# Rotating an 8192 x 8192 matrix: the last macro tile divided by rows, its loads emitted ahead of its outputs

## Chip, cores, metric

One core of a Trainium2 chip. The metric is the device time of one execution in microseconds. Times are medians over executions unless a profile is named; a profile is one execution, and its own span is about 1.8 us shorter than the time that is counted for it. In the profiles PE is TensorE (PEld its weight loads), DVE is VectorE, ACT is ScalarE, POOL is GpSimd and SP is SyncE; "ACTq" is the part of ACT that issues transfers.

## The reference

```python
def setup_inputs():
    return {"x": np.random.randn(8192, 8192).astype(np.float32), "k": 1}

def reference(x, k):
    return np.rot90(x, k)
```

With k = 1 the output is out[i, j] = x[j, 8191 - i]: a transpose with the columns taken from right to left. 268 MB are read and 268 MB written, and no arithmetic is done.

## The kernel before

The matrix is handled in macro tiles of 1024 rows and 4096 columns. One macro tile is eight loads of 128 rows (2 MB each, 16 KB in a row). VectorE reverses the columns inside each block of 128 into chunks `ar`, PE transposes the blocks into PSUM (the memory that PE writes to), ACT copies two PSUM halves into an output tile, and ACT issues a store of 2 MB: 4 column blocks (G = 4), 128 partitions, rows of 1024 elements (4 KB).

```python
a_pool = tile_pool(bufs=2)      # load buffers, 16 KB a partition
r_pool = tile_pool(bufs=68)     # reversed chunks; a macro tile needs 64
o_pool = tile_pool(bufs=2)      # output buffers, 16 KB a partition
psum_pool = tile_pool(bufs=2, space=PSUM)
...
for r0, c0, C in tiles:
    last = (r0, c0, C) == tiles[-1]
    ...                          # eight loads into a_pool, VectorE copies into chunks[t, j]
    for g0 in range(0, C // P, G):
        if last and g0 // G % 2 == 0:
            ot = a_pool.tile([P, W], dt, tag="a")     # no load needs it any more
        else:
            ot = o_pool.tile([P, W], dt, tag="o")
        S = PW if last and g0 + G == C // P else G
        for h in range(0, G, PW):
            ps = psum_pool.tile([P, PW, R], f32)
            for w in range(PW):
                for t in range(RT):                   # all eight rows of blocks
                    nc.tensor.transpose(ps[:, PW - 1 - w, t * P : (t + 1) * P],
                                        chunks[t, ...], ident)
            nc.scalar.copy(o[:, G - PW - h : G - h, :], ps[:])
            if (h + PW) % S == 0:
                nc.scalar.dma_start(out=dst, in_=...)
```

(Cut; "..." marks what is left out.) An output group needs a block of every one of the eight loads. So the first store of a macro tile cannot start before the eighth load of it has landed and is reversed. In the middle of the run the stores of the tile before cover that wait. Behind the last tile nothing follows, and at its beginning the loads have ended.

## Time and profile before

| | before |
|---|---|
| time | 1271.75 us (1271.64 to 1271.89, 4 executions) |
| span of the profile | 1269.2 us (its execution took 1270.97 us) |
| DMA engines at 9 tenths or more | 39 of 40 slices |
| PE / ACT / VectorE busy | 56% / 37% / 28% |
| last load landed | 1218.00 us |
| first store of the last macro tile issued | 1225.15 us |

From the page of the profile of before: the line of busy engines, the transfer queues (packets, MB, share of the 16 DMA engines' time) and the chain of waits that ended last.

```profile
PE 708.7 (56%) x4096; PEld 668.1 (53%) x4096; DVE 355.2 (28%) x1024; ACT 467.2 (37%) x257; POOL 0.7 (0%) x6
...
q10 hardware_dynamic: 18576, 268.44, 49.8%
q1 hardware_dynamic: 18432, 268.44, 49.8%
...
DMA 78%; ACT 18%; DVE 1%; PE 1%; issue 1%; ACTq 0%; DVEq 0%
```

The stores (q10) and the loads (q1) share the 16 DMA engines and fill 99.6% of their time together. No compute engine is near its limit. A gain is to be sought in stretches in which the DMA engines have nothing to do.

Such stretches are at the end. The same profile in windows; the last three columns are PE's granted clock (as a share of its full speed), the mean busy share of the DMA engines and GB/s.

```profile
core 0: us, PE busy (x) PEld busy (x) DVE busy (x) ACT busy (x) POOL busy (x), PEclk, DMA share, GB/s
1200.00:1213.00 13.00, 5.84 (x32) 5.60 (x32) 4.01 (x12) 4.68 (x3) 0.00 (x0) 0.74 1.01 429
1213.00:1217.00 4.00, 0.98 (x7) 0.74 (x7) 0.00 (x0) 2.59 (x2) 0.00 (x0) 0.78 0.63 264
1217.00:1221.50 4.50, 2.93 (x14) 2.93 (x15) 2.77 (x8) 0.71 (x1) 0.00 (x0) 0.50 0.97 411
1221.50:1226.00 4.50, 4.29 (x37) 4.05 (x36) 0.00 (x0) 3.23 (x3) 0.00 (x0) 0.93 0.05 22
1226.00:1230.00 4.00, 3.43 (x32) 3.15 (x31) 0.00 (x0) 3.43 (x2) 0.00 (x0) 1.00 0.93 393
1230.00:1250.00 20.00, 17.10 (x148) 15.76 (x147) 0.00 (x0) 17.18 (x10) 0.00 (x0) 1.00 1.02 428
```

From 1221.5 to 1226 the engines moved 22 GB/s: a hole of about 4.5 us. What ACT, which makes and issues the stores, did there (start, duration, instruction, and in brackets how long ACT was idle before and what ended it):

```profile
1211.95 3.63 ACT L137 COPY ot<-ps 128x2048 f32<-128x2048 f32 x2 [6.19 <-DMA out_dram<-ot]
1215.62 0.55 ACTq L145 DMA_DIRECT2D out_dram<-ot  x1
1220.79 1.87 ACT L137 COPY ot<-ps 128x2048 f32<-128x2048 f32 x1 [5.20 <-PE ps L132]
1223.25 1.87 ACT L137 COPY ot<-ps 128x2048 f32<-128x2048 f32 x1 [0.60 <-PE ps L132]
1225.15 0.55 ACTq L145 DMA_DIRECT2D out_dram<-ot  x1
```

The store issued at 1215.62 is the last of the tile before. ACT then waits 5.20 us for PE, because PE waits for the last load (landed at 1218.00) and its reversal. The first store of the last tile is issued at 1225.15 and its packets start at 1226.4.

### The profile page before, as it was taken

To read this page: it belongs to the slowest core of one execution; us is meant where nothing else is said; L and a number is where in the kernel's file an instruction comes from. 1 tells how busy PE (TensorE), PEld (TensorE's weight loads), DVE (VectorE), ACT (ScalarE), POOL (GpSimd) and SP (SyncE) were. 2 spreads that over 40 slices of the span, in tenths; PEclk is the share of its full clock that TensorE was granted. 3 is DMA by queue.
4 is the path that set the end of the run, shared out by engine and by line. 5 is a ranking of instruction groups with operands and counts; after the bars stand their busy time and mean duration, and the time that the engine had idled before them with its cause. 6 is when DMAs were issued, how large, how long until landed. Compare 5 with 4: busy or idle time off the path is not lost.

```text
span 1269.2 us, 10385 instructions
## 1 busy us (share of the span) xinstructions
PE 708.7 (56%) x4096; PEld 668.1 (53%) x4096; DVE 355.2 (28%) x1024; ACT 467.2 (37%) x257; POOL 0.7 (0%) x6
## 2 busy tenths in 40 slices
PE   1465645655556555665566555564555555655564
PEld 0364545645555455554556545554555555545564
DVE  4422322232223222232223222332223322232210
ACT  0333334333433343333433333333433343333454
POOL 0000000000000000000000000000000000000000
PEclk9968687776777867767767677677676877768787
DMA  9999999999999999999999999999999999999989
GB/s 400 415 431 429 429 428 429 430 428 429 428 429 428 430 430 428 429 429 430 428 428 420 429 429 429 429 429 427 428 422 427 426 421 430 427 427 427 428 342 382
DMA packets 37057, 537.55 MB, mean 424 GB/s; under 512 B 4112, under 2 KB 4112, under 8 KB 4112
## 3 DMA queue, kind: packets, MB, share of 16 engines
q10 hardware_dynamic: 18576, 268.44, 49.8%
q1 hardware_dynamic: 18432, 268.44, 49.8%
q8 instruction: 32, 0.52, 0.2%
q14 instruction: 17, 0.14, 0.0%
HBM read 268.44 MB, written 268.44 MB: 423 GB/s over the span
## 4 chain that ended last, share of the span: by engine, by line
DMA 78%; ACT 18%; DVE 1%; PE 1%; issue 1%; ACTq 0%; DVEq 0%
DMA out_dram<-ot 72%; ACT ot L137 18%; DMA a<-in_x_dram 6%; DVE ar L111 1%; PE ps L132 1%; ACTq L145 0%; ACTq L137 0%; DVEq L111 0%
## 5 line engine op out<-in xcount | busy, mean ns | idle before, releaser
L132 PE MATMUL ps<-ident,ar 128*128 128x128 f32 x4096 | 708.7, 353 | 544.3 <-ACT ot L137 461.5
L132 PEld LDWEIGHTS ps<-ident,ar 128*128 128x128 f32 x4096 | 668.1, 188 | 584.6 <-ACT ot L137 492.4
L137 ACT COPY ot<-ps 128x2048 f32<-128x2048 f32 x256 | 465.9, 1869 | 747.0 <-DMA out_dram<-ot 724.2
L111 DVE COPY ar<-a 128x512 f32<-128x512 f32 x1024 | 355.2, 421 | 865.7 <-DMA a<-in_x_dram 731.6
L137 ACT ACT_TABLE_LOAD x1 | 1.3, 1283 | 41.1 <-DVE ar L111 41.1
masks.py:199 POOL TENSOR_SCALAR_AFFINE_SELECT ident<-ident 128x128 f32<-128x128 f32 x1 | 0.3, 292 | 0.1
masks.py:197 POOL MEMSET ident<- 128x128 f32 x1 | 0.2, 204 | 0.3 <-POOLq L164 0.3
L164 POOL MEMSET const-bfloat16-1.0<- 128x1 bf16 x1 | 0.1, 101 | 0.0
L164 POOL MEMSET const-uint8-127<- 128x1 uint8 x1 | 0.1, 101 | 0.0
L164 POOL MEMSET const-float32-0.0<- 128x1 f32 x1 | 0.1, 98 | 0.2 <-issue 0.2
L164 POOL MEMSET const-float32-1.0<- 128x1 f32 x1 | 0.1, 98 | 0.0
## 6 DMA issues: line engine op xcount, KB each, us to landing
a<-in_x_dram SPq DMA_DIRECT2D x128, 2048.0 KB, 16.8
out_dram<-ot ACTq DMA_DIRECT2D x127, 2048.0 KB, 15.8
out_dram<-ot ACTq DMA_DIRECT2D x2, 1024.0 KB, 12.6
```

Source lines behind the costliest of these rows:

```text
L111: nc.vector.tensor_copy(out=ar[:], in_=a[:, u, j * CH : (j + 1) * CH].rearrange("r (b m) -> r b m", m=P)[:, :, ::-1],)
L132: nc.tensor.transpose(ps[:, PW - 1 - w, t * P : (t + 1) * P], chunks[t, g * P // CH][:, g % (CH // P), :], ident,)
L137: nc.scalar.copy(o[:, G - PW - h : G - h, :], ps[:])
L164: nc = _bacc.Bacc("TRN2", target_bir_lowering=False, num_devices=1)
```

## The change

The intent: divide the last macro tile into 768 and 256 rows, so that the first part's outputs need only six of the eight loads, and so go out while the last two land. All eight loads are emitted first, so that no load waits for a buffer that an output took. Outputs of the last tile use output and load buffers in turn, now beginning with an output buffer. The core of the diff (cut):

```diff
-LAST = [4096]
+LAST = [6, 2]
 ...
-    for r0, c0, C in tiles:
-        last = (r0, c0, C) == tiles[-1]
+    def load(r0, rt, c0):          # rt loads and their reversals
+    def store(r0, rt, c0, chunks, end, first):
+        rows = rt * P              # 1024, 768 or 256
+        PW = 1
+        while 2 * PW * rows <= FP: PW *= 2
+        G = PW
+        while 2 * G * rows <= F: G *= 2
 ...
-            if last and g0 // G % 2 == 0:
+            if end and (i + first) % 2 == 0:
                 ot = a_pool.tile(...)
 ...
+    *most, before_last, last = tiles
+    for m in most:
+        store(*m, load(*m), False, 0)
+
+    c1 = load(*before_last)        # rows 0..767 of the tile
+    c2 = load(*last)               # rows 768..1023
+    store(*before_last, c1, True, 1)
+    store(*last, c2, True, 1)
```

The first part gives eight stores of 1.5 MB in rows of 3 KB (ACT copies of 128x1536), the second one store of 2 MB and two of 1 MB in rows of 1 KB. Up to the last store of the tile before, the order of instructions on every engine is what it was.

More of the change, by code (lines that the diff above doesn't have):

```diff
@@ L16 @@
 RT = R // P
-LAST = [4096]
+LAST = [6, 2]
 W = 4096
 CH = 512
-G = 4
-PW = 2
+F = 4096
+FP = 2048
 def whole_reads(nc):
@@ L47, in macro_tiles @@
 def macro_tiles(N, M):
-    for r0 in range(0, N, R):
-        widths = [W] * (M // W)
-        if r0 + R == N:
-            widths[-1:] = LAST
-        c0 = 0
-        for C in widths:
-            yield r0, c0, C
-            c0 += C
+    tiles = [(r0, RT, c0) for r0 in range(0, N, R) for c0 in range(0, M, W)]
+    r0, _, c0 = tiles.pop()
+    for n in LAST:
+        tiles.append((r0, n, c0))
+        r0 += n * P
+    return tiles
 @with_exitstack
@@ L83 @@
     )
-    tiles = list(macro_tiles(N, M))
     loads = 0
-    for r0, c0, C in tiles:
-        last = (r0, c0, C) == tiles[-1]
-        q = W // C
+    def load(r0, rt, c0):
+        nonlocal loads
         chunks = {}
-        for t0 in range(0, RT, q):
+        for t in range(rt):
             if loads < RT and loads % 4 >= 2:
@@ L98 @@
             loads += 1
-            a = a.rearrange("r (q c) -> r q c", q=q)
             nc.sync.dma_start(
-                out=a,
-                in_=x[r0 + t0 * P : r0 + (t0 + q) * P, c0 : c0 + C].rearrange(
-                    "(q r) c -> r q c", q=q
-                ),
-            )
-            for u in range(q):
-                for j in range(C // CH):
-                    ar = r_pool.tile([P, CH // P, P], dt, tag="ar")
-                    nc.vector.tensor_copy(
-                        out=ar[:],
-                        in_=a[:, u, j * CH : (j + 1) * CH].rearrange(
-                            "r (b m) -> r b m", m=P
-                        )[:, :, ::-1],
-                    )
-                    chunks[t0 + u, j] = ar
@@ L119 @@
-        for g0 in range(0, C // P, G):
-            if last and g0 // G % 2 == 0:
-                ot = a_pool.tile([P, W], dt, tag="a")
-            else:
-                ot = o_pool.tile([P, W], dt, tag="o")
-            o = ot.rearrange("m (g f) -> m g f", g=G)
-            S = PW if last and g0 + G == C // P else G
+                out=a[:], in_=x[r0 + t * P : r0 + (t + 1) * P, c0 : c0 + W]
+            )
+            for j in range(W // CH):
+                ar = r_pool.tile([P, CH // P, P], dt, tag="ar")
+                nc.vector.tensor_copy(
+                    out=ar[:],
+                    in_=a[:, j * CH : (j + 1) * CH].rearrange(
+                        "r (b m) -> r b m", m=P
+                    )[:, :, ::-1],
+                )
+                chunks[t, j] = ar
@@ new lines, in load @@
+        return chunks
+    def store(r0, rt, c0, chunks, end, first):
+        rows = rt * P
+        PW = 1
+        while 2 * PW * rows <= FP:
+            PW *= 2
+        G = PW
+        while 2 * G * rows <= F:
+            G *= 2
+        for i, g0 in enumerate(range(0, W // P, G)):
+            if end and (i + first) % 2 == 0:
+                ot = a_pool.tile([P, F], dt, tag="a")
+            else:
+                ot = o_pool.tile([P, F], dt, tag="o")
+            o = ot[:, : G * rows].rearrange("m (g f) -> m g f", g=G)
+            S = PW if end and r0 + rows == N and g0 + G == W // P else G
@@ L127 @@
             for h in range(0, G, PW):
-                ps = psum_pool.tile([P, PW, R], mybir.dt.float32)
+                pt = psum_pool.tile([P, FP], mybir.dt.float32, tag="ps")
+                ps = pt[:, : PW * rows].rearrange("m (g f) -> m g f", g=PW)
                 for w in range(PW):
                     g = g0 + h + w
-                    for t in range(RT):
+                    for t in range(rt):
                         nc.tensor.transpose(
@@ L136 @@
                         )
-                nc.scalar.copy(o[:, G - PW - h : G - h, :], ps[:])
+                nc.scalar.copy(o[:, G - PW - h : G - h, :], ps)
                 done = h + PW
@@ L141 @@
                     top = M - c0 - (g0 + done) * P
-                    dst = out[top : top + S * P, r0 : r0 + R].rearrange(
+                    dst = out[top : top + S * P, r0 : r0 + rows].rearrange(
                         "(g m) f -> m g f", g=S
@@ L147 @@
                     )
+    tiles = macro_tiles(N, M)
+    *most, before_last, last = tiles
[5 more added lines that the diff above has]
+    store(*last, c2, True, 1)
 _INS = ['x', 'k']
```

## The prediction

> **What bounds the kernel now.** The transfers. The page's slices show the DMA engines at 9 tenths or more in 39 of 40 slices, at about 428 GB/s; PE is busy 56%, ACT 37%, DVE 28%; the chain of waits is 78% DMA. The Trainium skill ("DMA: Bandwidth & Descriptors", "Where 436 GB/s comes from") puts the ceiling of the 16 engines at 435 GB/s; this trace agrees with 428 to 430 in steady slices. 537 MB at 428 GB/s is about 1255 us of the 1269.2 us span, so no schedule can win over about 14 us (1.1%).
>
> **The loss at the end.** In one-microsecond windows the queues run full to about 1213.5 us, about half full from 1214 to 1218 (last load dripping in), full to 1221.7, near empty until 1226.3, then full to 1266; a straggling engine's packets end at 1267.8. The hole is 4.6 us. By the timeline: the last load lands at 1218.00, VectorE reverses it, PE transposes at half clock, ACT copies end at 1225.1, and only then is the last tile's first store issued (1225.15; its packets start at 1226.4).
>
> **What the change does.** The order of instructions on each engine up to the last store of the tile before is the same. The first part needs only six of the eight loads, the sixth landed at 1198.4, so its first store no longer waits for the last load. It waits for an output buffer instead: that of the second-last store of the tile before, landing at 1219.83. Then two ACT copies of 128x1536 instead of 128x2048: the big ones take 1.87 us, I estimate 1.44 us (by elements, with 0.16 us fixed). First new store issued at about 1222.8, packets at about 1224.0, 2.4 us earlier. The straggling engine ends the store before at about 1224.3, so on it about 2 us are won. The half-rate stretch stays.
>
> After that a 1.5 MB store takes about 3.67 us at 428 GB/s, and ACT's cadence is about 3.46 us (4.31 us now, less two times 0.43): just enough to keep the queue fed. Output buffers come in turn from both pools and are free in time.
>
> **What it costs.** The last 4 MB go out in rows of 1 KB, 12 MB in rows of 3 KB, instead of 4 KB. The skill (same page, "Specifications") asks for at least 512 B; no run here shows 1 KB yet. Loads with 16 KB rows take 611 ns a 16 KB packet, stores of 4 KB rows 615, so the cost of a row seems small; I estimate 0.2 to 1 us in all. Two more store issues (0.55 us) on ACT hide behind the queue.
>
> **Sum.** 1271.8 - 2.1 + 0.4 = 1270.1 us. 8 in 10: 1268.3 to 1272.0. Chances: faster by over 2% 0.003, within 2% 0.99, slower 0.007.
>
> **What would show it.** The first 128x1536 copy starts at about 1219.9, its wait ended by a landing store, not by PE; first new store near 1222.8; near-empty windows only from 1221.7 to 1224; 430 GB/s after; packets of the last three stores at 615 to 650 ns.
>
> **What would make it wrong.** Slow 1 KB rows (packets of 700 ns or more: the gain is gone); PE at half clock, so that ACT waits for it and the queue runs dry between the 1.5 MB stores; the straggling engine carrying its lag to the end, so that little is won.

## The result, and the profile after

| | before | changed |
|---|---|---|
| first measurement | 1271.75 us (1271.64 to 1271.89, 4) | 1270.13 us (1270.06 to 1271.06, 4) |
| again, on another chip | 1271.07 us (1270.39 to 1272.25, 9) | 1270.28 us (1269.53 to 1271.32, 5) |

The ratio is 0.9989 with a 95% interval of 0.9972 to 1.0006, and 0.9993 (0.9980 to 1.0005) the second time. A ratio is the mean time of one kernel's fast runs over that of the other's fast runs of the same rounds, so not quite the ratio of the medians above. Both intervals contain 1: by times alone the gain of about 1 us is not separated from the spread between executions. What happened inside has to be read from the traces.

The profile of the changed kernel is that of its slowest execution (1271.06 us; its span is 1269.2 us, as before, so this pair of profiles shows no gain in time). The same windows:

```profile
1200.00:1213.00 13.00, 5.74 (x37) 5.26 (x35) 3.71 (x11) 4.96 (x3) 0.00 (x0) 0.87 1.01 425
1213.00:1217.00 4.00, 3.40 (x16) 3.40 (x17) 0.00 (x0) 2.31 (x2) 0.00 (x0) 0.58 0.49 205
1217.00:1221.50 4.50, 1.39 (x12) 1.16 (x11) 2.77 (x8) 1.80 (x2) 0.00 (x0) 0.88 0.96 408
1221.50:1226.00 4.50, 4.50 (x23) 4.50 (x22) 0.00 (x0) 2.42 (x2) 0.00 (x0) 0.50 0.57 240
1226.00:1230.00 4.00, 3.64 (x27) 3.34 (x25) 0.00 (x0) 2.71 (x2) 0.00 (x0) 0.84 0.58 246
1230.00:1250.00 20.00, 16.83 (x143) 15.40 (x144) 0.00 (x0) 15.90 (x13) 0.00 (x0) 1.00 1.01 420
...
1254.00:1261.00 7.00, 1.18 (x11) 0.94 (x9) 0.00 (x0) 3.46 (x2) 0.00 (x0) 0.79 1.04 390
```

The hole is half filled: 240 GB/s instead of 22. But the next window fell from 393 to 246, and 1254 to 1261 runs at 390 where before it had 422 (that line of before is not shown). ACT tells why the next window fell:

```profile
1219.70 2.78 ACT L147 COPY ot<-pt 128x1536 f32<-128x1536 f32 x2 [4.39 <-DMA out_dram<-ot]
1222.52 0.55 ACTq L155 DMA_DIRECT2D out_dram<-ot  x1
1224.05 1.44 ACT L147 COPY ot<-pt 128x1536 f32<-128x1536 f32 x1 [1.57 <-PE pt L142]
1226.61 1.44 ACT L147 COPY ot<-pt 128x1536 f32<-128x1536 f32 x1 [1.12 <-PE pt L142]
1228.08 0.55 ACTq L155 DMA_DIRECT2D out_dram<-ot  x1
```

As predicted, the first copy starts when a store lands and frees its buffer (1219.70; 1219.9 was predicted), and the first store is issued at 1222.52 (1222.8 predicted; 1225.15 before). Then ACT waits for PE twice, because PE's clock stood at 0.50 from 1220.44 to 1227.27 in this execution. The second store is issued 5.6 us after the first, whose transfer takes only about 3.7 us, and a second hole opens: no packet of a store starts between 1227.34 and 1229.29 us.

### One more way to look at the end: the last of 16 engines

A transfer is spread over the 16 DMA engines, and its semaphore gets one increment from each. The Trainium skill ("DMA: Bandwidth & Descriptors", "Why a DMA increments its semaphore by 16 and not by 1") says that only the full 16 means that all data has landed; this trace shows how far apart the 16 can be. The last load of before had 8 of its increments by 1210.94 us, 14 by 1213.70, 15 by 1215.66, and the last at 1218.00. The stretch from 1213 to 1217 at 264 GB/s is made of this: the engines run out of work one after another (the store issued at 1205.79 landed between 1214.23 and 1219.83).

So the useful interval for this change is from the landing of the last store of the tile before (on its last engine) to the landing of the very last store (on its last engine). It leaves out what differs between executions earlier. It is read from the times of the semaphore increments in each trace (the median engine is the mean of the 8th and the 9th):

| kernel (one profile each) | last store of the tile before | last store, median engine | last store, last engine | interval to the last engine |
|---|---|---|---|---|
| before | 1224.86 | 1266.39 | 1268.24 | 43.38 |
| a4, not divided | 1225.07 | 1267.57 | 1269.47 | 44.40 |
| changed, profile above | 1224.59 | 1267.19 | 1268.11 | 43.52 |
| a1, changed again | 1224.41 | 1265.73 | 1266.72 | 42.31 |
| a2, PE kept busy | 1225.23 | 1266.59 | 1267.46 | 42.23 |
| b3, 512 and 512 | 1224.98 | 1265.53 | 1267.11 | 42.13 |
| b4, 896 and 128 | 1225.03 | 1266.22 | 1267.06 | 42.03 |
| a3, load buffer first | 1225.04 | 1264.67 | 1265.87 | 40.83 |
| c3, short rows in 1 MB stores | 1224.94 | 1263.99 | 1265.40 | 40.46 |
| c2, 512 and 512, load buffer first | 1225.17 | 1262.91 | 1265.25 | 40.08 |
| c1, two groups divided | 1224.65 | 1262.28 | 1264.67 | 40.02 |
| c4, more instructions | 1234.72 | 1276.47 | 1277.57 | 42.85 |

The 16.8 MB of the last tile at 428 GB/s are 39.2 us, an estimate from the steady windows: about the least that this interval can be, if the engine that is last at its start does a sixteenth of the tile. In before and a4 the first store waits for the last load alike, and their intervals differ by 1.0 us, so a difference of that size between two single profiles shows little.

### The profile page after: what moved, and what is told of

The parts are those of the page before. It is cut to its first block, busy times and chain, and to the rows that moved or that the text cites. A ratio compares the mean times of both kernels' runs of the same rounds, so it can differ in the third digit from the quotient of the medians.

```text
span 1269.2 us, 10394 instructions
## 1 busy us (share of the span) xinstructions
PE 710.7 (56%) x4096; PEld 670.7 (53%) x4096; DVE 355.1 (28%) x1024; ACT 467.6 (37%) x261; POOL 0.7 (0%) x6
## 4 chain that ended last, share of the span: by engine, by line
DMA 77%; ACT 18%; PE 2%; DVE 1%; issue 1%; ACTq 0%; SPq 0%; DVEq 0%
DMA out_dram<-ot 68%; ACT ot L147 18%; DMA a<-in_x_dram 10%; PE pt L142 2%; DVE ar L106 1%; ACTq L155 0%; SPq L101 0%; ACTq L147 0%; DVEq L106 0%
## 5 line engine op out<-in xcount | busy, mean ns | idle before, releaser
L142 PE MATMUL pt<-ident,ar 128*128 128x128 f32 x4096 | 710.7, 353 | 544.5 <-ACT ot L147 468.7
L142 PEld LDWEIGHTS pt<-ident,ar 128*128 128x128 f32 x4096 | 670.7, 189 | 584.3 <-ACT ot L147 499.6
L147 ACT COPY ot<-pt 128x2048 f32<-128x2048 f32 (+1 forms) x260 | 466.4, 1843 | 748.8 <-DMA out_dram<-ot 727.8
## 6 DMA issues: line engine op xcount, KB each, us to landing
a<-in_x_dram SPq DMA_DIRECT2D x128, 2048.0 KB, 16.8
```

Of the source, the lines that this page charges most:

```text
L142: nc.tensor.transpose(ps[:, PW - 1 - w, t * P : (t + 1) * P], chunks[t, g * P // CH][:, g % (CH // P), :], ident,)
L147: nc.scalar.copy(o[:, G - PW - h : G - h, :], ps)
```

## The experiments

Theory at the start: the first store no longer waits for the last load, which wins about 2 us; short rows cost something back; in some executions PE's clock opens a second hole. Rivals: the order of the buffers wins and not the division; the emission order of the loads does not matter; and the end is set not by the sum of the engines but by the one that is behind.

### a1: the changed kernel again

No edit.

> The changed kernel once more, to see its spread. In the profile on record a second gap opened behind the first new store (1227.4 to 1229.2 us), because PE ran at half clock from 1220.4 to 1227.3; that execution took 1271.06 us, the other three 1270.06 to 1270.19. Theory (PE's clock is granted in windows of 3.41 us whose phase differs by execution): executions fall in two groups, near 1270.1 without the second gap and near 1271.0 with it. Rival (one profile was taken in a slow moment): all executions near 1270.1, whatever the clock does in the profile.

Measured: 1270.28 us (1269.53, 1269.67, 1270.28, 1270.84, 1271.32); the kernel before spread as much in the same rounds (1270.39 to 1272.25). The profile:

```profile
1219.50 2.78 ACT L147 COPY ot<-pt 128x1536 f32<-128x1536 f32 x2 [3.75 <-PE pt L142]
1222.32 0.55 ACTq L155 DMA_DIRECT2D out_dram<-ot  x1
1223.04 2.78 ACT L147 COPY ot<-pt 128x1536 f32<-128x1536 f32 x2 [0.75 <-PE pt L142]
1225.85 0.55 ACTq L155 DMA_DIRECT2D out_dram<-ot  x1
```

Here PE had full clock from 1219.98 us on, the second store followed the first by 3.5 us, and there is no second hole. (The first wait is put down to PE, but the copy started 0.07 us after the buffer's store had landed at 1219.43.) The interval of the table is 42.31 us against 43.52 in the first profile, so the second hole may cost about 1.2 us where it occurs; two single profiles do not show the size. The two groups of executions that were expected are not there; the five times are spread over the whole range. That the clock alone makes the spread is not shown.

### a2: PE kept busy across its wait

```diff
-                for w in range(PW):
+                again = 3 if end and rt == LAST[0] and g0 == 0 and h == PW else 1
+                for w in list(range(PW)) * again:     # the same values once more
```

> The changed kernel; the second half of the first new store repeats its 16 transposes (12 of them here) three times, same values, while PE would be idle between 1218 and 1221 us. Clock theory: PE stays at or comes to full clock before 1224, ACT does not wait for PE at the second new store, the gap at 1227 to 1229 is gone in the profile, and the time is 1270.1 us or less in every execution. Rival (the second gap is the DMA's own, from issue to first packet): the gap stays. If the DMA engine that lags behind the others sets the end, no more than about 1 us is won over the changed kernel's slow executions and nothing over its fast ones.

Measured: 1270.35 us (1270.22 to 1271.55), ratio to before 0.9996 (0.9982 to 1.0010). In its profile PE's clock is full from 1218.86 us on and the second hole is gone (interval 42.23). Against the changed kernel's executions nothing is won that the times could show. The second hole is real, but these times do not show that it is what separates the executions.

### a3: load buffer first

```diff
-    store(*before_last, c1, True, 1)
+    store(*before_last, c1, True, 0)
```

> The changed kernel, but the first new store takes the load buffer (of the seventh load, reversed at about 1211 us) and the second the output buffer, the other way round. Its first copy can then start at about 1216 instead of 1219.7, its store is issued at about 1219.3 instead of 1222.5, so its packets are there before the store before it ends on most engines (1221.2). Theory 1 (what counts is the hole as seen in the sum of all engines): 2.0 to 2.5 us faster than the changed kernel, about 1267.8. Theory 2 (the end is set by the one DMA engine that is behind, and that one has work until about 1224.0 in any case): the hole in the sum closes, but the time is that of the changed kernel's fast executions, 1269.8 to 1270.1.

Measured: 1268.59 us (1267.91 to 1269.33), ratio to before 0.9979 (0.9966 to 0.9991). In the same rounds the changed kernel had 1270.28, so this is 1.7 us better than it (its slowest execution is faster than the changed kernel's fastest, 1269.53) and 2.5 better than before, and its interval excludes 1. From its profile, ACT and then the windows of the old hole:

```profile
1215.64 0.55 ACTq L155 DMA_DIRECT2D out_dram<-ot  x1
1216.38 1.44 ACT L147 COPY ot<-pt 128x1536 f32<-128x1536 f32 x1 [0.77 <-PE pt L142]
1218.43 1.44 ACT L147 COPY ot<-pt 128x1536 f32<-128x1536 f32 x1 [0.61 <-PE pt L142]
1219.91 0.55 ACTq L155 DMA_DIRECT2D out_dram<-ot  x1
```

```profile
1217.00:1221.50 4.50, 4.24 (x32) 3.76 (x30) 2.78 (x8) 3.21 (x3) 0.00 (x0) 0.87 0.97 408
1221.50:1226.00 4.50, 3.35 (x28) 3.07 (x29) 0.00 (x0) 3.81 (x4) 0.00 (x0) 1.00 0.95 399
1226.00:1230.00 4.00, 3.41 (x31) 3.12 (x30) 0.00 (x0) 3.33 (x3) 0.00 (x0) 1.00 1.05 434
```

ACT goes on 0.77 us after the store of the tile before, since the seventh load's buffer has been free since its reversal at about 1211. The old hole is closed. So in the changed kernel the wait for the last load was replaced by a wait for an output buffer, and the buffer order decided it. Neither theory hit the size: 1268.59 lies between the 1267.8 of the sum of the engines and the 1269.8 to 1270.1 of the last engine. The landings show how. In a1 the engines resumed nearly together (first new store: median engine 1227.70, last 1228.18). Then a packet of 16 KB on the queue that fetches instructions took 0.92 us from 1231.70, and the last landing, 0.8 us behind the median at the second new store, was 2.0 us behind at the third. In a3 the others kept a lead of 2.9 us (1225.98 and 1228.83). A fetch of 0.92 us at 1229.98 moved the 15th landing from 1.2 to 2.0 us behind the median, and the last one stayed at 2.9. So the delay vanished in the lead, as far as one profile of each can show.

The edit also makes something worse. The first part now ends with an output buffer, and the second part begins with one again, so ACT waits for a landing once more (ACT in a3's profile):

```profile
1247.84 3.64 ACT L147 COPY ot<-pt 128x2048 f32<-128x2048 f32 x2 [3.75 <-DMA out_dram<-ot]
```

The first store of the second part is issued 7.4 us after the store before it (1244.12 and 1251.51), PE's clock falls to 0.50 from 1248.88 to 1255.71, and from 1251 to 1253 the engines moved 279 GB/s. c2 and c3 inherit this edit (waits of 1.1 and 2.3 us in c2, 2.9 and 3.8 in c3); c1 has no such wait of over 0.6 us. A version of a3 with buffers in turn throughout was not run.

### a4: not divided

```diff
-LAST = [6, 2]
+LAST = [8]
...
-    c1 = load(*before_last)
-    c2 = load(*last)
-    store(*before_last, c1, True, 1)
-    store(*last, c2, True, 1)
+    c1 = load(*last)
+    store(*last, c1, True, 1)
```

> The last macro tile left whole (1024 rows), with the changed kernel's order of buffers (output buffer first). If the division is what wins, its first store waits for the last load as before (issued at about 1225) and the time is that of the kernel before, 1271.7 us, ratio 1.000. If the order of buffers is what wins, it is 1270.1 like the changed kernel.

Measured: 1271.35 us, ratio 1.0001 (0.9989 to 1.0014), as expected: without the division the new order of buffers wins nothing, since the first store (issued at 1226.35) waits for the last load in any case. It is later than the 1225.15 of before because PE stood at half clock until 1224.77 in this profile and until 1222.10 in that of before. So the clock can shift either kernel by about a microsecond, as far as these single profiles show.

### b1: loads not emitted ahead

```diff
     c1 = load(*before_last)
-    c2 = load(*last)
     store(*before_last, c1, True, 1)
+    c2 = load(*last)
     store(*last, c2, True, 1)
```

> The changed kernel, but the last part's two loads are emitted after the first part's outputs. Their load buffers are then taken by outputs in between, so these loads wait for stores of the first part to land and come late; after the last load the queues have nothing left to do until it is landed, reversed, transposed and copied, estimated from this case's durations at about 9 us (2 landing, 0.5 reversal, 1.9 transposes, 3.7 two copies, 1.2 issue to first packet). Theory (the emission ahead is a necessary part of the change): 6 to 12 us slower than the changed kernel, 1276 to 1282 us. Rival (the scheduler orders by readiness, the emission order in the program hardly matters): within 1 us of the changed kernel.

Measured: 1282.93 us, ratio to before 1.0092 (1.0077 to 1.0107), slower than expected by a little. Its profile, first what the load queue waited for after 1200 us, then the windows around the last load (landed at 1259.0):

```profile
SPq L101 <- DMA out_dram<-ot: 68.8, 3, 34.1
```

```profile
1240.00:1258.00 18.00, 0.89 (x2) 0.36 (x2) 2.77 (x8) 0.00 (x0) 0.00 (x0) 0.50 0.91 352
1258.00:1267.00 9.00, 7.08 (x48) 6.80 (x49) 2.77 (x8) 3.64 (x2) 0.00 (x0) 0.73 0.01 2
```

The loads wait for stores, and behind the last load is a hole of 9 us, as estimated. The loads emitted ahead are a necessary part of the change: without them the divided kernel is about 12 us slower than the one before.

### b2: output buffers only

```diff
-            if end and (i + first) % 2 == 0:
+            if end and rt != LAST[0] and (i + first) % 2 == 0:
```

> The changed kernel, but the first part's outputs use the two output buffers only, not the load buffers in turn. A buffer is then held for two copies (2.8), the issue (0.6) and about 6.3 us from issue to landing, so two stores take about 9.8 us instead of 7.3. Theory (four buffers are needed to keep the queue full once loads have ended): about 8 us slower than the changed kernel, 1276 to 1280 us. Rival (two buffers are enough, stores overlap): within 1 us.

Measured: 1275.39 us, ratio to before 1.0032 (1.0017 to 1.0047): about 5 us slower than the changed kernel (by way of the kernel before, since the changed one did not run in these rounds) where 8 were expected, so the direction is right and the size was overestimated. What ACT waited for between 1221 and 1262 us (total, times, longest), here and then in the changed kernel:

```profile
ACT ot L147 <- DMA out_dram<-ot: 17.2, 9, 4.4
```

```profile
ACT ot L147 <- DMA out_dram<-ot: 4.4, 1, 4.4
```

With two buffers every one of the first part's stores waits for a landing. The third ingredient, buffers in turn, is needed as well.

### b3: 512 and 512 rows

`LAST = [4, 4]`, nothing else.

> The changed kernel with the last macro tile divided 512 and 512: all 16 MB in rows of 2 KB, as many rows (8192) as with 768 and 256. Its first store has copies of 128x2048, so it is issued about 0.9 us later. In the profiles so far packets are slow for about 6 us from the moment the first store with 1 KB rows is issued, and go well after (325 ns for 8 KB). Theory (the cost is that of making many row descriptors, in the time they are made): packets are somewhat slower all through the 16 MB, and the time is 1270.5 to 1272. Rival (only rows as short as 1 KB cost): packets of 615 to 625 ns throughout, and 1269.5 to 1270.5.

Measured: 1269.94 us, ratio 0.9991 (0.9976 to 1.0006). The packets of 16 KB took 631 ns on average from 1228 us on (median 625, nine in ten under 666; 623 on average in before), with no stretch as slow as in the changed kernel. The time is in the rival's range, so the number of rows (8192 in both) is not what makes packets slow; that they are 1% slower throughout fits the theory as well.

### b4: 896 and 128 rows

`LAST = [7, 1]`, nothing else.

> The changed kernel with the last macro tile divided 896 and 128: 14 MB in rows of 3.5 KB and the last 2 MB in rows of 512 B, again 8192 rows. Theory (the making of the descriptors costs): the last 2 MB carry as many rows as the last 4 MB of the changed kernel, in half the bytes, so that they take 8 to 10 us instead of 5; 1271 to 1274 us, slower than the changed kernel by 1 to 3. Rival (the cost goes by bytes in short rows): half the cost of the changed kernel, 1269.5 to 1270.3.

Measured: 1270.26 us, ratio 0.9994 (0.9977 to 1.0011). The last 2 MB in rows of 512 B ran at 692 ns per 16 KB on average, and the packets before them at 625 ns on average although the issue of the last store took 6.87 us. This too speaks against the making of descriptors as the cause, and agrees with the rival. The three divisions cannot be told apart by their times.

### c1: only two column groups divided

```diff
-    c1 = load(*before_last)
-    c2 = load(*last)
-    store(*before_last, c1, True, 1)
-    store(*last, c2, True, 1)
+    c = load(r0, RT, c0)
+    store(r0, 6, c0, c, True, 0, 0, (0, 8))        # column blocks 0..7, 768 rows
+    store(r0, RT, c0, c, True, 0, 0, (8, 20))      # whole
+    store(r0, 2, c0, c, True, 1, 6, (0, 8))        # the remaining 256 rows of blocks 0..7
+    store(r0, RT, c0, c, True, 0, 0, (20, 32))     # whole
```

(`store` gets two more arguments, the first row block and the range of column blocks.)

> Load buffer first, as in the experiment that won most so far; and only the first two of the eight column groups are divided into 768 and 256 rows. The other six go out whole in rows of 4 KB, since by then the last load is reversed. The two groups' 256-row remains (1 MB in rows of 1 KB instead of 4 MB) go out in the middle. Theory (the short rows cost, about 2 us on most DMA engines and about 0.5 on the last one): faster than the load-buffer-first kernel by 0.3 to 1.5 us, 3 to 4 us faster than the kernel before. Rival (short rows cost nothing on the engine that sets the end): the same as load buffer first, 2.5 us faster than the kernel before.

Measured: 1267.54 us (1267.38 to 1267.90), before in these rounds 1270.81, ratio 0.9975 (0.9963 to 0.9988): about 3.2 us by that ratio, within what was expected. The end of its profile:

```profile
1221.50:1226.00 4.50, 3.92 (x35) 3.52 (x33) 0.00 (x0) 3.79 (x3) 0.00 (x0) 1.00 1.03 429
1226.00:1230.00 4.00, 3.79 (x33) 3.46 (x32) 0.00 (x0) 3.33 (x3) 0.00 (x0) 1.00 1.01 417
1230.00:1250.00 20.00, 16.93 (x145) 15.57 (x144) 0.00 (x0) 16.96 (x10) 0.00 (x0) 1.00 1.00 418
...
1254.00:1261.00 7.00, 0.00 (x0) 0.00 (x0) 0.00 (x0) 0.00 (x0) 0.00 (x0) 0.50 0.98 412
```

No hole is left, and 1254 to 1261 runs at 412 instead of 390 GB/s. Its interval, 40.02 us, is 0.8 above the floor. It has the lowest median found; none of its executions is as slow as any of the kernel before or of the changed one, though it did not run in the same rounds as the changed kernel. In its own rounds its slowest execution is faster than the fastest of c3 (1268.28), which has the load buffer first and divides all groups. That the longer rows win this is not shown, since c3 also has the late waits for buffers that c1 lacks.

### c2: 512 and 512 rows, load buffer first

The edits of b3 and a3 together.

> 512 and 512 rows (2 KB rows, packets near 630 ns throughout in the earlier run), with the load buffer first. The gain of the buffer order and that of the longer rows should add: 2.5 to 3.3 us faster than the kernel before, 0 to 0.8 faster than 768 and 256 with the load buffer first. Rival (they do not add, as the same engine is last in any case): 2.5 us or less.

Measured: 1267.97 us (1267.53 to 1269.17), ratio to before 0.9981 (0.9968 to 0.9993), so 2.4 us by the ratio and 2.8 by the medians. That is on the border between the two expectations; whether the longer rows add to the buffer order is not settled by this run.

### c3: the short rows in stores of 1 MB

```diff
-        while 2 * G * rows <= F:
+        while 2 * G * rows <= F and rt != LAST[1]:
```

together with the edit of a3.

> 768 and 256 rows, load buffer first, but the 256-row part goes out in four stores of 1 MB (8 rows of 1 KB a partition) instead of one of 2 MB (16 rows) and two of 1 MB. In the profiles the slow packets (16 KB at 710 to 870 ns) are those around the 2 MB store with 16 rows, the 1 MB ones take 325 ns for 8 KB. Theory (the slow stretch belongs to the 2 MB store with 16 rows): it is gone, all packets of the last 4 MB take about 325 ns, and most engines end 1 to 1.5 us earlier. Rival (it belongs to the making of row descriptors while earlier stores still drain): packets are slow for as long as before, whatever the stores' size.

Measured: 1268.50 us, ratio to before 0.9983 (0.9969 to 0.9996), so no better than a3's 0.9979. But the slow stretch is gone. In the changed kernel the 16 KB packets of the 2 MB store, 16 rows of 1 KB each, take 710 ns on average and up to 913 (769 and 1075 in a1); here the packets of the last 4 MB take 644 ns per 16 KB on average, and none more than 808. So the stretch belongs to that store's form. Why 16 rows of 1 KB in a packet do this, and why packets of the store before it (rows of 3 KB) are slowed too after it is issued (510 ns instead of 473 from 1254 to 1255 in the changed kernel), stays open.

That the time is not better has two possible reasons, which this run does not separate. One is the last engine: the slow stretch falls on engines that are ahead. In a1 the last 4 MB took 11.8 us on the median engine (1253.94 to 1265.73) and 10.5 on the last one (1256.20 to 1266.72), against an estimated 9.8 at 428 GB/s. The other is that ACT waited 3.8 us for a buffer before the last two stores, so that from 1257 to 1258 the engines moved 98 GB/s.

### c4: 4096 more instructions on an idle engine

```diff
+    junk = consts.tile([P, 1], dt)
+    for _ in range(4096):
+        nc.gpsimd.memset(junk, 0.0)
```

> The changed kernel plus 4096 memsets of one 128x1 tile on the idle POOL at the start. They touch nothing else, but their instructions have to be fetched: 4096 of 64 bytes are 256 KB, 16 more packets of 16 KB beside the 32 there now, each about 1 us on one DMA engine. Theory (an engine that serves a fetch falls behind and stays behind, and the engine that is last sets the end): slower than the changed kernel by 1 us if the fetches fall on the engines in turn, by up to 10 us if they fall on one or two. Rival (fetches are lost in the noise of the traffic): within 0.3 us.

Measured: 1278.75 us (1276.91 to 1280.52), ratio to before 1.0062 (1.0049 to 1.0074): 8 to 9 us slower than the changed kernel. The memsets lie between 1 and 757 us. Windows of this profile, then the same of the changed kernel, then the fetch queue of each in the same order:

```profile
300.00:600.00 300.00, 172.66 (x947) 164.13 (x948) 83.27 (x240) 109.07 (x60) 205.34 (x1640) 0.73 1.01 419
900.00:1200.00 300.00, 175.05 (x982) 166.38 (x983) 86.05 (x248) 111.56 (x62) 0.00 (x0) 0.75 1.01 429
```

```profile
300.00:600.00 300.00, 174.33 (x987) 164.97 (x985) 86.00 (x248) 109.59 (x61) 0.00 (x0) 0.72 1.01 429
900.00:1200.00 300.00, 175.19 (x982) 166.99 (x983) 85.06 (x246) 109.77 (x61) 0.00 (x0) 0.73 1.01 427
```

```profile
q14 instruction: 49, 0.40, 0.1%
```

```profile
q14 instruction: 18, 0.14, 0.0%
```

While POOL runs, the same loads and stores move at 419 instead of 429 GB/s; when it has ended, the rates are equal. Compute engines are about as busy as without. The fetches added 0.26 MB, a 2000th of the traffic, in 31 packets of 8 KB. At 0.31 us a packet (their duration in the trace) these are 9.6 us if one engine serves them all and 0.6 us if all 16 share them. The measured 8 us fit one engine, or two that share them unevenly, which the whole transfer then waits for.

The landings of the loads support this. The last engine is 0.9 us behind the median on average in the first 100 us and 9.1 us behind from 400 to 500 (3.3 in the changed kernel). The rate holds at 428 GB/s from 100 to 300 us, while the lag grows, and is 416 from 400 to 500; when the memsets have ended, the lag falls to 3.3 us (900 to 1000). POOL is as busy in the one stretch as in the other, so its running as such is not what slows the transfers. The table adds that the last tile itself takes no longer (42.85 us): all is lost before it. In the packets the loss shows as loads and stores of over 700 ns, 346 of them from 300 to 600 us against 11 in the changed kernel. The trace does not name the engine of a packet, so that the fetches fall on one engine or two is argued, not seen.

## Why the prediction was right

- **The bound and the class.** The transfers are the limit, the change touches only the end, and the result is within 2%. Right.
- **The gain.** First new store at 1222.8 predicted, 1222.52 and 1222.32 measured; its cause, a landing store instead of PE, and the copies of 1.44 us are as predicted (with 1.87 us for 2048 elements, they give 0.15 us that does not depend on the size; 0.16 was put in). By the times the changed kernel won 1.6 us in the first measurement and 0.8 in the second. By the table the interval shrank from 43.38 (before; 44.40 in a4) to 42.31 in a1, so 1.1 to 2.1 us, of which the cost of short rows is already taken off; 1.7 net was predicted. The profile itself has 43.52. Right, within what so few executions can tell.
- **Near-empty windows only from 1221.7 to 1224, then 430 GB/s.** Wrong in the first profile: a second hole from 1227.3 to 1229.3, from PE at half clock. The prediction named that as a way to fail, without putting it into the sum. a1's profile does not have it, and its interval is 1.2 us shorter. That the profile shows no gain is probably due to it. Nor were there 430 GB/s after: 420 from 1230 to 1250 and 390 from 1254 to 1261 in that profile.
- **The cost of short rows, "0.2 to 1 us in all".** The term was mis-sized on most engines and right on the one that counts. Packets of the 2 MB store took 710 ns on average in the first profile and 769 in a1, not 615 to 650 (those of the two 1 MB stores, 650 per 16 KB in the median, did); on the median engine the last 4 MB took 2.0 us more than at the steady rate in a1, on the last engine 0.7.
- **The straggling engine.** It was read correctly as what limits the gain ("on it about 2 us are won"). The prediction treated it as a constant of the run. a3 and c4 show more: it is not one fixed lag, for which landing is last can change when an engine is held up, and the lead of the others can hide their own delays.
- **The total, 1270.1 us.** That it met 1270.13 so closely is luck: executions of one kernel differ by more than 1 us, and the second hole and the slower packets were not in the sum.

Where did the rest of the 4.5 us hole go? About 2 us of it stayed, because the first new store waits for an output buffer; a3 took that away with one character (and opened a smaller hole later). And what the hole in the sum of engines shows is not all to be won, because one engine is working in it.

## What to carry to other kernels

When a transfer-bound kernel runs dry at its end, divide the last piece so that its first output needs less input, emit all its loads first, and give the outputs the buffers in the order in which they become free, not simply in turn: on top of the division, the order of buffers was worth more here (1.7 us) than the division in the form that was tried (about 1); without the division an order of buffers won nothing (a4). Check the order across the seam of the two parts as well, where a3 lost some of it. Dividing only as much as is needed to bridge the wait (two of eight groups) gave the lowest median; whether by its longer rows is not shown. Read a transfer's landing as that of its slowest engine: a hole in the mean of 16 engines can be work for one of them.

## What the Trainium skill lacked or had wrong

- "Runtime: NRT & Kernel Launch", "Instruction fetch mechanics", says that crossing a 16 KiB boundary of instructions is mostly hidden. In this transfer-bound kernel 4096 instructions on an idle engine (16 such boundaries) cost about 8 us of 1270 (c4), probably since the fetches take time on the DMA engines that the transfers wait for: the lag of the last engine grew to 9.1 us.
- "TensorE: Matmul & The Clock Gate", "Part 4: PE-mode transpose", says that the full clock does not engage for transposes in PE's transpose mode. Here PE does nothing but such transposes, of fp32, and the granted clock was 1.00 for 34 us on end in the profile of before (1222.10 to 1256.23) and 37.6 us in a1. Its window of about 3.4 us (Part 1) does show: the stretches of one clock last 3.41 us or multiples of it.
- "DMA: Bandwidth & Descriptors", "Specifications", gives 512 B as the least transfer for line rate. Stores took 615 ns per 16 KB with rows of 4 KB, about 630 with 2 KB, 650 with 1 KB and 692 with 512 B; and a 2 MB store with 16 rows of 1 KB in a packet ran at 710 to 769, which stores with 8 such rows did not (644 in c3).
- No page puts a number on how far the 16 engines of one core drift apart in a long run. The last engine was 1.3 us behind the median landing on average, loads and stores together, in the first 100 us of before and 4.8 us from 900 to 1200 us, at most 7.0.
